# Fixed places for a residual's loads, and other steps of a two-layer trunk moved in time

## The chip, the cores and the metric

The kernel runs on one core of a Trainium2 chip. The metric is device time of one execution in microseconds (us), as the median of three runs. The engines are PE (TensorE, matrix products, with its weight loads PEld), DVE (VectorE), ACT (ScalarE), POOL (GpSimd) and SP (SyncE, which here issues all transfers). Each works through its own instructions in the order in which they were written; they wait for one another by semaphores. PSUM is the memory that PE writes to, in banks of 128 x 512 float32.

## The reference

A trunk of two layers over 1024 tokens of width 1024, all float32. Layer 0 mixes by gated linear attention, layer 1 by sparse attention with a learned index. The change touches layer 1 only. Its core:

```python
# dsa_mixer: 16 heads of 128, 8 index heads of 64, topk = 256, blocks of 128 queries
q = apply_partial_rope(h[..., :o1].reshape(B, L, DSA_HEADS, DSA_HEAD_DIM), cos_h, sin_h)
z = h[..., o3:o4]
rel = relu(einsum('bthd,bsd->bths', qi_b, ki))
score = einsum('bths,bth->bts', rel, wi_b) * INDEX_SCALE      # causal ones only
_, idx = lax.top_k(score, topk)
logits = einsum('bthd,btjd->bthj', q_b, gather(k, idx)) * ATTN_SCALE
o = einsum('bthj,btjd->bthd', softmax(logits), gather(v, idx))
y = (o * silu(z)) @ w_out
# the trunk, after either mixer
x = layer_norm(ALPHA * x + y, ln_g[i], ln_b[i])
x = x + (p[i] @ ple_w[i]) * sigmoid(x @ ple_gate_w[i])
```

All heads share one key and one value of width 128. The top 256 of each query's scores are not gathered: a threshold per query is searched for, and scores below it are masked in `bias_t`.

## The kernel before

**Products in parts.** PE multiplies float32 in three passes: each operand is split in a high and a low part, and a group is high x high, high x low, low x high. The high part is made by ACT (L393, `q<-qf`, `x<-xst`, `u<-uf`; for weights L173, for the probabilities `ph<-PT` at L1463), the low part by DVE behind it (L385; L1461 for `PT`). The layer's weights were split earlier and kept in memory, and come as pairs of transfers `whi`, `wlo` (L165).

**Stages of layer 1.** At 1065 us its projections for keys, values and index begin, then the scores. The tokens are then done in two halves of 512 (half 0 from about 1121 us, half 1 from about 1540). A half consists of 17 slots, numbered -1 to 15, of about 19 to 21 us each. Slot h has as its spine whole blocks of projections (`q` or `z` of a head to come, or an output block `dsa_out` that adds into `y`), and the attention of head h is interleaved: logits `S`, their exponentials into `sq` (ACT, L1417), a turn by DVE (L1423), four stores `sqd` to memory and a load `PT` back in another layout (SP, L1436 and L1446), the split of `PT`, and its products with the values into `o`. A row of sums goes to memory and comes back as `inv`; `uf` is `o` times gate `z` times `inv` (L1515), and its split `u` feeds the output blocks. Behind slot 15 come the last output blocks (`last_outs`), the layer norm of each group of 128 tokens (statistics L795, apply L800, then transposes by PE at L62), and the tail with `p` and the gate (`ple`, `gx`).

**The residual.** `y` starts as alpha times x, which lies transposed in memory (`x2s`, eight tiles of 128 x 512). A tile is loaded into one of two buffers `xst` (L1343), turned by four PE transposes into a PSUM bank from the pool `pb` of three banks (L62), and copied by ACT into `y` (L1370). The loads run one ahead of the transposes. Half 1's input `X` comes by the same loader (`feed_x2`), split instead of turned.

**Top-k.** For the four largest blocks of queries a search bit by bit runs on while half 0 goes: counts on DVE (L1032, 640 to 1024 columns) and, for three blocks, as sign passes on ACT (L1076). The three blocks' scores `sc` are stored first (L1054, `sc_s<-sc`) and read back for the last bit (L1069, `sc<-sc_s`).

**What sets the order.** The program that writes the instructions keeps a clock `fl.now` of planned PE time. `Flow.run` writes the spine and after each piece calls `pace`, which writes every step whose planned time has come (`fl.at`, `after`, `chain`) and lets the pacers step: the weights' loads, and `Background` objects that take one step of a generator each `gap` planned us. `bg` does the top-k, `bg2` the residual. `fl.need(condition)` writes steps ahead of their time until the condition holds. Loads of `p` and their splits are `load_p` (splits `wait` planned us later); the loads of X for half 1 step by `feed_by(feed_x2(X, 1), first time, gap)`.

Of the kernel before, what the change touches and what calls it, by code (L numbers as in the profile page):

```python
# [23 lines left out]
HT = 512  # L24
# [23 lines left out]
class Flow:  # L48
# [23 lines left out]
    def chain(self, *steps):  # L72

        (_, first), rest = steps[0], steps[1:]
        first()
        if rest:
            self.after(rest[0][0], lambda: self.chain((0, rest[0][1]), *rest[1:]))
# [177 lines left out]
def trunk_kernel(ctx, tc, x_tok, x_T, p_T, pos, freq, g_q, g_k, g_v, g_z, g_a, g_a2, g_ba, g_gn, g_o,  # L255
# [79 lines left out]
    later = [key for key, _ in small_keys()] + list(dict.fromkeys(  # L335
        key for key, _ in seq if key[0] in ("dq", "dz", "do") or key[:2] in (("p", 1), ("t", 1))))
    W = Weights(nc, wp, seq, dp, fl.after)
    bg, bg2, bg3 = Background(), Background(), Background()
    fl.pacers += [W.pace, bg.pace, bg2.pace, bg3.pace]


    negs = cp.tile([128, 128], F32, name="negs")
# [38 lines left out]
    def pbank():  # L381
        return psum[0].tile([128, 512], F32, tag="pb", name="pb", bufs=psum[1])
# [4 lines left out]
    def split(hi, lo, src, done=None):  # L387

        def second():
            lo_part(lo, src, hi)  # L390
            if done:
                done()
        chain((0, lambda: act.activation(hi, src, AF.Copy)), (0.9, second))  # L393
# [377 lines left out]
    def load_p(layer, half, alloc, wait=3.0):  # L771
        P = []
        for k in range(2):
            st = xp.tile([128, HT], F32, tag="xst", name="xst", bufs=2)
            nc.sync.dma_start(st, p_T[layer, k, :, half * HT:half * HT + HT])
            ph, pl = alloc(), alloc()
            after(wait, lambda ph=ph, pl=pl, st=st: split(ph, pl, st))
            P.append((ph, pl))
        return P
# [107 lines left out]
    swap_h = list(range(16, 32)) + list(range(16))  # L887
    swap_i = list(range(8, 16)) + list(range(8)) + list(range(16, 32))

    def rope(x, c, s, swap, tmp, then):  # L890
        ab = []

        def first():
            ab[:] = tmp()[:x.shape[0]], tmp()[:x.shape[0]]
            a, b = ab
            dve.tensor_mul(b, x, c)
            dve.stream_shuffle(a, x, swap)
            dve.tensor_mul(a, a, s)

        def second():  # L900
            dve.tensor_add(x, *ab)
        chain((0, lambda: None), (0.8, first), (1.6, second), (1.2, then))


    def small_head(half, X, f32t, alloc, qalloc, tmp, spsum, kih, kil, res):
# [402 lines left out]
    def small_tile(tag, dt=F32, bufs=2):  # L1308
        return l1.tile([128, HT], dt, tag=tag, name=tag, bufs=bufs)
# [4 lines left out]
    def q_phase(st, h, X):  # L1314
        def ev(ps):
            qf = small_tile("qf")
            fl.need(lambda: h < 2 or st.get(("A", h - 2)) == 3)
            qh, ql = small_tile("q", F32R, 4), small_tile("q", F32R, 4)

            def done():  # L1320
                st["q", h] = qh, ql
            act.activation(qf, ps, AF.Copy)
            rope(qf[0:32], tabs[0], tabs[1], swap_h, tmp2, lambda: split(qh, ql, qf, done))

        yield from fm_block(("dq", h), X, ev)

# [30 lines left out]
                X.put(*got)  # L1357
            yield

    def residual(y, rows):  # L1360
        for got in rows:
            if got:
                by_token(y, *got)
            yield

    def by_token(y, k, st):
        ps = pbank()
        for t in range(4):
            fl.transpose(ps[:, t * 128:t * 128 + 128], st[:, t * 128:t * 128 + 128], ident)
        act.activation(y[:, :, k * 128:k * 128 + 128], ps.rearrange("p (t c) -> p t c", c=128), AF.Copy,  # L1370
                       scale=ALPHA)

    def attend(st, h, half, ap, sq):

# [149 lines left out]
                                     [store(i) for i in range(nb)], [load(i) for i in range(nb)], [inverse, to_all])]  # L1524

    def dsa_out(st, js, ch, y, norm=None, ahead=1):
        parts = [W.take(("do", j, ch)) for j in js]

        def U(t, b):
            h = 2 * js[0] + b  # L1530
            fl.need(lambda: ("u", h) in st)
            return tuple(x[:, t * 128:t * 128 + 128] for x in st["uhl", h])

        yield from accumulate(parts, U, y, ch, None, norm, ahead)
        if ch:
            st["out"] = 2 * js[-1] + 2
# [23 lines left out]
    def start_topk(n=len(steps)):  # L1560
        fl.req(res.get("n", 0) == n)
        tk = lambda: sp.tile([128, L], F16, tag="tk", name="tk", bufs=2)
        bg.set(topk_steps([4, 5, 6, 7], scs, l1, tk, tk, on_act=(1, 2, 3)), 1.65)
    fl.at(fl.now + 55.0, start_topk)
    v0, v1 = (vT[i][:, 4:].rearrange("p t d -> p (t d)") for i in range(2))
    raw = xp.tile([128, 4, D], F32, tag="y", name="y").rearrange("p a (b t) -> p (a b) t", t=HT)
# [26 lines left out]
    def unit(u, norm=None):  # L1593
        if u[0] == "o":
            return dsa_out(st, u[1], u[2], y, norm, 3 if u == last_outs[1] else 1)
        return (q_phase if u[0] == "q" else dz_phase)(st, u[1], X)

    for half in range(NH):
# [11 lines left out]
        for h, units in enumerate(plan, -1):  # L1610
# [25 lines left out]
                    fl.at(start + 13.0, loads[0])  # L1636
            last_dur = dur
            if h == 15:
                Pt = load_p(1, half, lambda: small_tile("q", F32R, 4), 8.0)
            if h == -1:  # L1640
                rows = x2_tiles(half)
                next(rows)
            elif h == 0:
                y = xp.tile([128, 4, D], F32, tag="y", name="y")
                bg2.set(residual(y, rows), 4.6 if half else 3.3)
            elif h == 4:
                bg2.finish()
            fl.run(*(unit(u) for u in units))
        norm, y_done = norm_steps(y, l1)
        if half == 0:  # L1650
            X = XT()
            feed_by(feed_x2(X, 1), fl.now + 5.0, 3.0)
        for u in last_outs:
            fl.run(unit(u, norm if u == last_outs[-1] else None))
        fl.drain()
        st.clear()
# [74 lines left out]
```

## Time and profile before

| | us |
|---|---|
| median of three runs (2041.94 to 2046.78) | 2044.94 |
| profiled execution | 2044.36 |
| its span in the trace | 2042.6 |
| PE busy in it | 1971.9 |
| DVE busy | 1489.5 |
| ACT busy | 1040.1 |
| mean share of the transfer engines of SP's queue | 67.9% |

Busy times are sums over the span; PE's idle time is the difference to the span, and the view of waits says which semaphore ended it. The granted clock of PE stands beside the windows: 1.00 is 2.4 GHz, a value between 0.5 and 1 is a mean over a window in which part ran at 1.2 GHz. In timelines consecutive instructions of one kind on the same tiles are drawn together (x2), with their summed duration, and the bracket gives idle time before the first and what ended it.

### The profile page before, as it was taken

How to read it: one execution, taken by the hardware profiler on the slowest of the kernel's cores; microseconds unless marked ns; L12 is line 12 of the kernel's file. 1: busy time of each engine (PE TensorE's matmuls, PEld its weight loads, DVE VectorE, ACT ScalarE, POOL GpSimd, SP SyncE). 2: the span in 40 equal slices, each digit the busy share in tenths (PEclk: the TensorE clock that was granted, in tenths of full speed). 3: DMA queues.
4: the chain of work that ended last, by engine and by line, in shares of the span. 5: the costliest groups of instructions: out<-in, count | busy, mean ns of one | idle time of the engine just before them, and what ended most of it. 6: DMA issues, size and time to landing. Idle time of an engine off the chain costs nothing.

```text
span 2042.6 us, 26801 instructions
## 1 busy us (share of the span) xinstructions
PE 1971.9 (97%) x9016; PEld 1616.1 (79%) x9016; DVE 1489.5 (73%) x3037; ACT 1040.1 (51%) x1943; POOL 88.5 (4%) x151
## 2 busy tenths in 40 slices
PE   8899999999899999999999999999999999999999
PEld 6678888887777788888788777888778887878877
DVE  5676666686777787877857978677696887777873
ACT  5564645445465646464445656666432554434432
POOL 0110101010001101010100000000000000000000
PEclk9999999999999999999999999999999999999999
DMA  4457574757856465656557487878856988888774
GB/s 147 172 155 223 167 224 164 223 171 257 286 187 224 146 218 169 223 168 217 179 192 271 152 278 256 302 257 283 276 190 227 333 314 292 299 294 302 256 266 145
DMA packets 173946, 464.96 MB, mean 228 GB/s; under 512 B 20080, under 2 KB 20848, under 8 KB 167664
## 3 DMA queue, kind: packets, MB, share of 16 engines
q1 hardware_dynamic: 173808, 463.25, 67.9%
q8 instruction: 71, 1.16, 0.2%
q14 instruction: 67, 0.55, 0.1%
HBM read 331.18 MB, written 131.99 MB: 227 GB/s over the span
## 4 chain that ended last, share of the span: by engine, by line
PE 75%; DVE 11%; DMA 6%; ACT 5%; issue 2%; SPq 1%; POOLq 0%; ACTq 0%; POOL 0%; DVEq 0%
PE pb L58 55%; PE o L58 7%; PE U L58 6%; PE S L58 5%; DVE wlo L175 1%; DMA wls<-pst 1%; DVE bn L795 1%; DVE sq L1423 1%; DMA sqd<-sq 1%; DMA whi<-whs 1%; DMA xst<-x2s 1%; DMA PT<-sqd 1%; ACT tk L1076 1%; DMA y<-in_x_T 1%; PE oT L62 1%
## 5 line engine op out<-in xcount | busy, mean ns | idle before, releaser
L58 PE MATMUL pb<-x,whi 128*128 128x512 f32 x2272 | 712.5, 395 | 3.7 <-ACT whi L173 2.3
L58 PEld LDWEIGHTS pb<-x,whi 128*128 128x128 f32 x2272 | 418.1, 189 | 84.4 <-ACT whi L173 3.2
L58 PE MATMUL pb<-x,wlo 128*128 128x512 f32 x1136 | 445.1, 392 | 0.5 <-DVE wlo L175 0.5
L58 PE MATMUL pb<-whi,u 128*128 128x512 f32 x1024 | 345.9, 397 | 5.7 <-ACT u L393 4.2
L58 PEld LDWEIGHTS pb<-x,wlo 128*128 128x128 f32 x1136 | 214.3, 189 | 48.7 <-DVE wlo L175 2.7
L175 DVE TENSOR_TENSOR wlo<-wst,whi 128x512 fp32r<-128x512 f32 x296 | 198.2, 686 | 63.1 <-ACT whi L173 62.7
L58 PEld LDWEIGHTS pb<-whi,u 128*128 128x128 f32 x1024 | 193.6, 189 | 47.8 <-ACT u L393 4.8
L173 ACT ACTIVATE whi<-wst 128x512 fp32r<-128x512 f32 x296 | 174.9, 622 | 78.9 <-DMA wst<-in_g_o 19.8
L58 PE MATMUL pb<-wlo,u 128*128 128x512 f32 x512 | 201.6, 394 | 0.0
L209 ACT ACTIVATE phi<-pst 128x512 fp32r<-128x512 f32 x130 | 81.5, 627 | 138.5 <-DMA pst<-in_d_z 34.1
L1417 ACT ACTIVATE sq<-P,mx 128x128 f32<-128x128 f32 (+7 forms) x128 | 99.0, 773 | 86.6 <-DVE mx L1410 60.1
L58 PE MATMUL S<-kT,q 128*128 128x512 f32 (+2 forms) x576 | 122.5, 344 | 0.6 <-DVE q L385 0.6
L1463 ACT ACTIVATE ph<-PT 128x512 fp32r<-128x512 f32 (+1 forms) x160 | 92.7, 601 | 53.5 <-PE o L58 38.4
L1461 DVE TENSOR_TENSOR PT<-PT,ph 128x512 fp32r<-128x512 f32 (+1 forms) x160 | 101.8, 648 | 21.9 <-ACT ph L1463 21.9
L58 PEld LDWEIGHTS S<-kT,q 128*128 128x128 f32 x576 | 100.2, 189 | 19.4 <-DVE mx L1410 1.7
L58 PEld LDWEIGHTS pb<-wlo,u 128*128 128x128 f32 x512 | 97.1, 190 | 18.4
L1076 ACT ACTIVATE tk<-sc,tki 128x768 f16<-128x768 f32 (+2 forms) x90 | 92.8, 1032 | 27.1 <-DVE tki L1085 20.9
L58 PE MATMUL o<-ph,vT 128*128 128x512 f32 (+2 forms) x384 | 101.6, 349 | 4.0 <-ACT ph L1463 4.0
L213 DVE TENSOR_TENSOR pst<-pst,phi 128x512 fp32r<-128x512 f32 x130 | 89.7, 690 | 20.3 <-ACT phi L209 20.2
L1423 DVE STREAM_TRANSPOSE sq<-sq 128x128 f32<-128x128 f32 (+7 forms) x128 | 97.8, 769 | 6.6 <-ACT sq L1417 6.4
L58 PE MATMUL pb<-whi,x 128*128 128x512 f32 x256 | 90.0, 410 | 10.5 <-ACT whi L173 6.1
L1410 DVE CUSTOM_DVE_ANT_0 P<-S,bias 128x512 f32<-128x512 f32 (+3 forms) x128 | 71.2, 561 | 21.1 <-PE S L58 16.7
(311 smaller groups left out, 3282.4 us busy)
## 6 DMA issues: line engine op xcount, KB each, us to landing
whi<-whs SPq DMA_DIRECT2D x130, 512.0 KB
wlo<-wls SPq DMA_DIRECT2D x130, 512.0 KB
sqd<-sq SPq DMA_DIRECT2D x192, 256.0 KB
PT<-sqd SPq DMA_DIRECT2D x48, 1024.0 KB
whs<-phi SPq DMA_DIRECT2D x130, 256.0 KB
wls<-pst SPq DMA_DIRECT2D x130, 256.0 KB
wst<-in_g_v SPq DMA_DIRECT2D x32, 512.0 KB
wst<-in_g_z SPq DMA_DIRECT2D x32, 512.0 KB
```

Source lines behind the costliest of these rows:

```text
L58: self.pe.matmul(out, lhsT, rhs, start=start, stop=stop)
L62: self.pe.transpose(out, in_, ident)
L173: self.nc.scalar.activation(hi[:, c], st[:, c], AF.Copy)
L175: self.nc.vector.tensor_sub(lo[:, c], st[:, c], hi[:, c].bitcast(F32))
L209: self.nc.scalar.activation(hi, st.bitcast(F32), AF.Copy)
L213: self.nc.vector.tensor_sub(st, st.bitcast(F32), hi.bitcast(F32))
L1076: act.activation(junk()[:, :n], scs[j], AF.Sign, bias=cand[:, j:j + 1].bitcast(F32), accum_out=cnt[:, j:j + 1])
L1410: dve.tensor_tensor_reduce(P[:, a:a + e], ps[:, :e], bias_t[T][:, a:a + e], op0=OP.add, op1=OP.min, scale=-ATTN_SCALE, scalar=lim, accum_o ...
L1417: act.activation(to, rows, AF.Exp, scale=-1.0, bias=mx, accum_out=sm[:, t:t + 1])
L1423: dve.transpose(x, x)
L1461: dve.tensor_sub(lo, lo.bitcast(F32), hi.bitcast(F32))
L1463: chain((0, lambda: act.activation(hi, lo.bitcast(F32), AF.Copy)), (0.8, second))
```

## The change

Five edits, all in layer 1:

1. The residual no longer runs as a background generator. In slots 0 to 3 of each half, two tiles are loaded at 2.2 and 2.8 planned us after the slot's start, and their transposes and copies stand 3.6 and 2.0 planned us before its end. An output block needs all eight first.
2. The split of a head's `q` stands 3.0 instead of 1.2 planned us behind the last step of its rotary (DVE L901).
3. The top-k steps every 1.6 instead of 1.65 planned us, and when the last output block begins it pauses for at least 11 planned us.
4. The splits of `p` stand 14 instead of 8 planned us behind their loads.
5. The loads of half 1's input begin 14 instead of 5 planned us behind the end of slot 15, every 2.8 instead of 3.0.

```diff
-        chain((0, lambda: None), (0.8, first), (1.6, second), (1.2, then))
+        chain((0, lambda: None), (0.8, first), (1.6, second), (wait, then))
...
-            rope(qf[0:32], tabs[0], tabs[1], swap_h, tmp2, lambda: split(qh, ql, qf, done))
+            rope(qf[0:32], tabs[0], tabs[1], swap_h, tmp2, lambda: split(qh, ql, qf, done), 3.0)
...
-    def residual(y, rows):
-        for got in rows:
-            if got:
-                by_token(y, *got)
-            yield
+    def residual(st, y, half, ks, start, end):
...
+        for i, k in enumerate(ks):
+            fl.at(start + 0.6 * i, lambda k=k: load(k))
+            fl.at(end - 3.6 + 1.6 * i, lambda k=k: by_token(k))
...
     def dsa_out(st, js, ch, y, norm=None, ahead=1):
+        fl.need(lambda: st.get("y") == NK)
...
-        bg.set(topk_steps([4, 5, 6, 7], scs, l1, tk, tk, on_act=(1, 2, 3)), 1.65)
+        bg.set(topk_steps([4, 5, 6, 7], scs, l1, tk, tk, on_act=(1, 2, 3)), 1.6)
...
-                Pt = load_p(1, half, lambda: small_tile("q", F32R, 4), 8.0)
-            if h == -1:
-                rows = x2_tiles(half)
-                next(rows)
-            elif h == 0:
+                Pt = load_p(1, half, lambda: small_tile("q", F32R, 4), 14.0)
+            if h == 0:
                 y = xp.tile([128, 4, D], F32, tag="y", name="y")
-                bg2.set(residual(y, rows), 4.6 if half else 3.3)
-            elif h == 4:
-                bg2.finish()
+            if 0 <= h < 4:
+                residual(st, y, half, (2 * h, 2 * h + 1), start + 2.2, start + dur)
...
-            feed_by(feed_x2(X, 1), fl.now + 5.0, 3.0)
+            feed_by(feed_x2(X, 1), fl.now + 14.0, 2.8)
         for u in last_outs:
+            if u == last_outs[-1]:
+                bg.due = max(bg.due, fl.now + 11.0)
             fl.run(unit(u, norm if u == last_outs[-1] else None))
```

How three places read in the order of the instructions. First SP's queue in slot 0 of half 0 (`xst<-x2s` are the residual's loads, `sc_s<-sc` stores of the top-k), before:

```order
L1343 DMA xst<-x2s 128x512
L1489 DMA inv<-row 128x512
L1436 DMA sqd<-sq 32x4x512 x4
L1054 DMA sc_s<-sc_9849 128x768
L165 DMA whi<-whs 128x1024
L165 DMA wlo<-wls 128x1024
L1054 DMA sc_s<-sc_9850 128x896
L1343 DMA xst<-x2s 128x512
L1054 DMA sc_s<-sc_9851 128x1024
L1446 DMA PT<-sqd 128x2048
```

and in the changed kernel:

```order
L1366 DMA xst<-x2s 128x512 x2
L1496 DMA inv<-row 128x512
L165 DMA whi<-whs 128x1024
L165 DMA wlo<-wls 128x1024
L1054 DMA sc_s<-sc_9849 128x768
L1443 DMA sqd<-sq 32x4x512 x4
L1054 DMA sc_s<-sc_9850 128x896
L1054 DMA sc_s<-sc_9851 128x1024
L1453 DMA PT<-sqd 128x2048
```

The slot's two residual loads now stand together, ahead of the stores of scores and of the four `sqd` stores; two of these stores of scores follow the `sqd` stores, and no residual load stands before `PT`.

Second DVE at the end of half 0, where its last attention head closes, from behind the split of the first `PT` of the piece on (`q<-xst` are the low parts of `p`, `x<-xst` of half 1's input, L1032 are counts of the top-k, 768 and more columns after the reload), before:

```order
L385 TENSOR_TENSOR q<-xst,q 128x512 x2
L1032 TENSOR_SCALAR tk,tkf<-sc_9848,tki 128x640
L754 TENSOR_TENSOR y<-pb,y 128x512
L1461 TENSOR_TENSOR PT<-PT,ph 128x4x96
L1082 TENSOR_TENSOR tki<-tkf 128x4
L1083 SCALAR_TENSOR_TENSOR tki<-tki 128x4
L1085 TENSOR_SCALAR tki<-tki 128x4
L1461 TENSOR_TENSOR PT<-PT,ph 128x2x4x64
L1506 TENSOR_TENSOR z<-z,inv 128x512
L1515 TENSOR_TENSOR uf<-o,z 128x4x4x32
L385 TENSOR_TENSOR x<-xst,x 128x512
L385 TENSOR_TENSOR u<-uf,u 128x512
```

and in the changed kernel, from behind the same `PT` on:

```order
L1072 TENSOR_SCALAR tki<-tki 128x3
L754 TENSOR_TENSOR y<-pb,y 128x512
L1468 TENSOR_TENSOR PT<-PT,ph 128x4x96
L1032 TENSOR_SCALAR tk,tkf<-sc_9848,tki 128x640
L1468 TENSOR_TENSOR PT<-PT,ph 128x2x4x64
L1032 TENSOR_SCALAR tk,tkf<-sc_9849,tki 128x768
L1513 TENSOR_TENSOR z<-z,inv 128x512
L1522 TENSOR_TENSOR uf<-o,z 128x4x4x32
L1032 TENSOR_SCALAR tk,tkf<-sc_9850,tki 128x896
L385 TENSOR_TENSOR q<-xst,q 128x512 x2
L385 TENSOR_TENSOR u<-uf,u 128x512
```

The low parts of `p` moved from behind the first `PT` to behind `uf`, half 1's input left the piece, and two counts of a later round now stand here, one of them between `uf` and the low part of `u`. On SP the three reloads that these counts read stood behind the loads of half 1's input; now the first stands right behind `inv`, and the other two one pair of weight loads later.

Third ACT in a slot of half 1 in which a head's `q` is made (`qf` is the copy from PSUM, `q<-qf` the high part, `ph<-PT` the probabilities' high parts), before:

```order
L1463 ACTIVATE ph<-PT 128x512 x2
L1322 ACTIVATE qf<-pb 128x512
L393 ACTIVATE q<-qf 128x512
L1463 ACTIVATE ph<-PT 128x512 x2
L1463 ACTIVATE ph<-PT 128x384
L1463 ACTIVATE ph<-PT 128x512
```

and in the changed kernel:

```order
L1470 ACTIVATE ph<-PT 128x512
L1322 ACTIVATE qf<-pb 128x512
L1470 ACTIVATE ph<-PT 128x512 x2
L393 ACTIVATE q<-qf 128x512
L1470 ACTIVATE ph<-PT 128x512
L1470 ACTIVATE ph<-PT 128x384
L1470 ACTIVATE ph<-PT 128x512
```

The split `q<-qf` stood right behind `qf`, with four `ph` behind it; now two `ph` stand between the two, and three behind.

## Rows read from the trace of the kernel before

**Rows 1.** section 1 of the page: engine, busy us, share, instructions

```profile
PE 1971.9 (97%) x9016; PEld 1616.1 (79%) x9016; DVE 1489.5 (73%) x3037; ACT 1040.1 (51%) x1943; POOL 88.5 (4%) x151
```

**Rows 2.** waits of PE, stretches 1150:1200, 1440:1540, 1660:1960, 1960:2043 in turn

```profile
PE pb L62 <- DMA xst<-x2s: 4.8, 1, 4.8
...
PE pb L58 <- ACT u L393: 2.7, 1, 2.7
PE S L62 <- DVE y L800: 2.4, 3, 1.5
PE o L58 <- DVE PT L1461: 1.5, 1, 1.5
...
PE o L58 <- ACT ph L1463: 4.0, 3, 1.8
...
PE pb L58 <- DVE y L754: 1.4, 1, 1.4
```

**Rows 3.** windows: us, busy of PE, PEld, DVE, ACT, POOL, clock, DMA share, GB/s

```profile
1180.00:1200.00 20.00, 15.20 (x73) 12.55 (x72) 12.80 (x34) 7.52 (x17) 0.00 (x0) 0.91 0.98 323
1460.00:1480.00 20.00, 15.74 (x60) 12.19 (x59) 12.17 (x23) 5.41 (x10) 0.00 (x0) 0.83 0.88 313
1480.00:1500.00 20.00, 17.50 (x76) 13.75 (x75) 19.28 (x41) 6.70 (x11) 3.85 (x8) 0.91 0.51 173
```

**Rows 4.** timeline of PE, slot 0: start, duration, group, idle before and releaser

```profile
1192.40 1.09 PE L62 MATMUL pb<-ident,xst 128*128 128x128 f32 x4 [4.80 <-DMA xst<-x2s]
1193.14 1.20 PE L58 MATMUL pb<-x,whi 128*128 128x512 f32 x2
...
1195.59 0.63 PE L58 MATMUL pb<-x,whi 128*128 128x512 f32 x2
```

**Rows 5.** timeline of SP's queue, slot 0 of half 0

```profile
1178.53 2.71 SPq L1436 DMA_DIRECT2D sqd<-sq  x4
...
1185.07 0.42 SPq L1343 DMA_DIRECT2D xst<-x2s  x1
```

**Rows 6.** ACT's copies of the residual, and its top-k passes (page, section 5)

```profile
L1370 ACT ACTIVATE y<-pb x16: 574/581/600, 1168.4 to 1653.3; 128x512 f32<-128x512 f32 x16
...
L1076 ACT ACTIVATE tk<-sc,tki 128x768 f16<-128x768 f32 (+2 forms) x90 | 92.8, 1032 | 27.1 <-DVE tki L1085 20.9
```

**Rows 7.** timeline of DVE, end of half 0

```profile
1463.98 1.29 DVE L385 TENSOR_TENSOR q<-xst,q 128x512 fp32r<-128x512 f32 x2
...
1469.09 0.69 DVE L1515 TENSOR_TENSOR uf<-o,z 128x512 f32<-128x512 f32 x1 [0.28 <-PE o L58]
...
1472.54 0.68 DVE L385 TENSOR_TENSOR u<-uf,u 128x512 fp32r<-128x512 f32 x1
```

**Rows 8.** timeline of ACT, end of half 0

```profile
1471.27 0.63 ACT L393 ACTIVATE x<-xst 128x512 fp32r<-128x512 f32 x1 [5.86 <-DMA xst<-x2s]
1471.80 0.61 ACT L393 ACTIVATE u<-uf 128x512 fp32r<-128x512 f32 x1
```

**Rows 9.** timeline of SP's queue, end of half 0

```profile
1460.90 0.33 SPq L1489 DMA_DIRECT2D inv<-row  x1
...
1464.70 0.98 SPq L1343 DMA_DIRECT2D xst<-x2s  x2
```

**Rows 10.** timeline of PE, end of half 0

```profile
1472.47 0.79 PE L58 MATMUL pb<-whi,u 128*128 128x512 f32 x1 [2.72 <-ACT u L393]
```

**Rows 11.** timeline of DVE, last norm of half 0

```profile
1487.92 1.01 DVE L1032 TENSOR_SCALAR_CACHE_REDUCE tk<-sc,tki 128x768 f16<-128x768 f32 x1
...
1492.16 1.14 DVE L1032 TENSOR_SCALAR_CACHE_REDUCE tk<-sc,tki 128x896 f16<-128x896 f32 x1
```

**Rows 12.** timelines of ACT and of PE, half 1

```profile
1686.49 0.63 ACT L393 ACTIVATE q<-qf 128x512 fp32r<-128x512 f32 x1 [5.37 <-DVE qf L901]
...
1687.69 0.73 PE L58 MATMUL o<-ph,vT 128*128 128x512 f32 x2 [1.78 <-ACT ph L1463]
```

**Rows 13.** instructions on tile S, PE, 1680 to 1720: min/median/max ns, first and last start

```profile
L58 PE MATMUL S<-kT,q x24: 278/362/397, 1696.4 to 1702.1; 128*128 128x512 f32 x12, 128*128 128x384 f32 x6, 128*128 128x256 f32 x6
```

More of the change, by code (lines that the diff above doesn't have):

```diff
@@ L337, in trunk_kernel @@
     W = Weights(nc, wp, seq, dp, fl.after)
-    bg, bg2, bg3 = Background(), Background(), Background()
-    fl.pacers += [W.pace, bg.pace, bg2.pace, bg3.pace]
+    bg, bg3 = Background(), Background()
+    fl.pacers += [W.pace, bg.pace, bg3.pace]
     negs = cp.tile([128, 128], F32, name="negs")
@@ L888, in trunk_kernel, with rope @@
     swap_i = list(range(8, 16)) + list(range(8)) + list(range(16, 32))
-    def rope(x, c, s, swap, tmp, then):
+    def rope(x, c, s, swap, tmp, then, wait=1.2):
         ab = []
@@ L1358, in feed_x2, with load, by_token @@
             yield
-    def residual(y, rows):
-        for got in rows:
-            if got:
-                by_token(y, *got)
-            yield
[L1366 to L1371, printed above, removed]
+    def residual(st, y, half, ks, start, end):
+        tiles = {}
+        def load(k):
+            tiles[k] = xp.tile([128, HT], F32, tag="xst", name="xst", bufs=2)
+            nc.sync.dma_start(tiles[k], x2s[k, :, half * HT:(half + 1) * HT])
+        def by_token(k):
+            ps = pbank()
+            for t in range(4):
+                fl.transpose(ps[:, t * 128:t * 128 + 128], tiles[k][:, t * 128:t * 128 + 128], ident)
+            act.activation(y[:, :, k * 128:k * 128 + 128], ps.rearrange("p (t c) -> p t c", c=128), AF.Copy,
+                           scale=ALPHA)
+            st["y"] = k + 1
+        for i, k in enumerate(ks):
+            fl.at(start + 0.6 * i, lambda k=k: load(k))
+            fl.at(end - 3.6 + 1.6 * i, lambda k=k: by_token(k))
     def attend(st, h, half, ap, sq):
```

## Prediction

> **What bounds the kernel now.** I read the busy shares first. TensorE (PE) is busy 1971.9 us of a span of 2042.6 us [rows 1], so only some 71 us of idle time can go, over both layers, and a faster kernel is one whose PE waits less or whose clock falls less. The change touches layer 1 alone (from about 1065 us on), so I then read the view of waits for PE there, stretch by stretch [rows 2]. Six lines are worth naming: one wait of 4.8 us of a transpose for the load of the residual, one of 2.7 us for `u`, three for the norm's `y` with 2.4 us, one of 1.5 us for `PT`, three for `ph` in half 1 with 4.0 us, and one of 1.4 us for `y` near the end. Then the table of 20 us windows: in layer 1 only a few show a granted clock below 1.00, among them the three printed [rows 3], where it is 0.91, 0.83 and 0.91. They hold the first four of these lines. So a wait there costs twice: itself, and matmuls at the lower of the two clock levels (1.2 instead of 2.4 GHz) right behind it. The timelines of these places give the terms below.
>
> **Residual in fixed places, slot 0 of half 0.** PE stands 4.80 us until 1192.40, for a tile `xst` [rows 4]. The order of SP tells why: the load was issued at 1185.07, behind four stores `sqd` (1178.53, 2.71 us of issuing) and stores of the scores [rows 5], with the transfer engines 98% busy at 323 GB/s [rows 3]. After the wait a pair of matmuls takes 1.20 us, and by 1195.59 a pair takes 0.63 again [rows 4]. Some 2.9 us thus ran at half speed, which costs 1.4 us. In the changed order the two loads of slot 0 stand before the scores' stores and the `sqd` stores, and their transposes stand at the slot's end, 3.6 and 2.0 planned us before it. The load then has over 10 us where it needed 7.3 (1185.07 to 1192.40). The wait goes, and with it the low clock: 4.8 + 1.4 = 6.2 us. The bounds: at most 6.2; at least 0, if the wait turns up at another load. The `PT` load behind them has fewer transfers ahead of it than before, so I see none that is late next.
>
> The same edit puts eight pairs of transposes (four slots in each half) at slot ends. PE's work is the same; ACT's copy takes 0.58 us [rows 6]. I count this as nothing, since PE has other matmuls between the two and before the slot's end, and ACT is half idle. If the cover fails, a slot's first matmul waits for a PSUM bank; that is the third rival.
>
> **The end of half 0.** Here four edits meet: p's splits later, half 1's loads later, and the top-k's reloads and counts, at a gap of 1.6 instead of 1.65, now ahead of them. Before, PE waits 1.54 us for `PT`, since VectorE (DVE) does two splits of `q` (1.29 us) and a count first [rows 7], and then 2.72 us for `u` until 1472.47 [rows 10]: ACT has done `u` only behind an `x` split whose load arrived at 1471.27 [rows 8], 6.6 us after SP began to issue it at 1464.70 [rows 9]. In the changed order of DVE `PT` comes ahead of the splits, so the 1.54 goes, and `u` on ACT is ahead of `x`. But before `u`'s low part DVE now does a count over 768 columns and one over 896, each of which waits for a reload, and the two `q` splits. Worked out with the 6.6 us: the 768 reload is issued behind `inv` (1460.90 [rows 9]) at about 1461.3 and is there at 1467.9; count 1.01 (as in [rows 11]), `z` and `uf` 1.3, so `uf` ends at 1470.2 where it ended at 1469.78 [rows 7]. The 896 reload, two weight loads later, is there at about 1470; count 1.14 [rows 11], splits 1.29, `u` 0.68 [rows 7]: `u` low is ready at about 1473.3. Before, that part began at 1472.54 and ended at 1473.2. PE thus resumes 1.7 us earlier, does two matmuls and waits again, and is past this place 0.3 us earlier or level. I take 0.3 us, and the low clock (0.83 over 1460 to 1480) stays. Bounds: a transfer 1.5 us later makes it a loss of 1; one that lands at once leaves only DVE's own work and brings `u` low to about 1472, a gain of 1.5, and 4.5 if the clock then holds.
>
> The row's 6.6 us is for 256 KB at a DMA share of 0.88. The Trainium skill (DMA: Bandwidth & Descriptors, Anatomy of one DMA) puts a transfer at about 2.0 us fixed plus its bytes over 436 GB/s, which by estimate is 2.6 us here and 3.1 us for the 896 reload; the trace does not agree, its queue is full. By that rule the end of half 0 would gain 1.5 instead of 0.3 us and the whole would come to 2031.3 us, part of the first rival.
>
> **The last norm of half 0.** Between statistics and applies DVE does top-k counts of 1.01 and 1.14 us [rows 11]; PE waits 2.4 us for `y` meanwhile [rows 2], and the clock of 1480 to 1500 is 0.91 [rows 3], which is up to 0.09 x 20 = 1.8 us. After, the pause keeps the top-k away until the applies are through: 2.15 us less on the chain that PE waits for. But DVE is busy 19.28 of 20 us there [rows 3], and the counts left over follow right behind. So I take the 2.4 us of waiting and nothing for the clock. Bounds: 4.2 (both), and 0 if the work comes back as waits behind the norm.
>
> **q's split later.** In three slots of half 1 ACT holds the split `q<-qf` for 5.37 us, waiting for DVE's rotary, with four `ph` queued behind it; PE waits 1.78 us at 1687.69 for the first of them [rows 12]. The lines of [rows 2] say 4.0 us in three. Now two `ph` stand between `qf` and the split. I take 3.5 us, leaving 0.5 for what remains of the late `ph`; bounds 0 and 4.0. Below nothing it does not go: `q` is first read at 1696.4 [rows 13], and its low split, two DVE instructions after 1687.69, has 7 us to spare before 1.8 us are added.
>
> These three waits come at a regular distance, one in about 106 us. The Trainium skill (Perfetto Trace Analysis, Identifying the Most-Contended Engine) says that a gap that repeats on the engine that should be full can mean too little SBUF or PSUM for the next tile. By that rule the order of ACT would not matter and the 3.5 us would stay: 2036.0 us, the second rival's upper neighbour. The trace speaks against it: ACT idles in the row, and what releases it is DVE.
>
> At the end of half 1 the wait of 1.4 for `y` [rows 2] loses the p splits (1.29) ahead of it, which now stand ahead of the last `PT` instead; I count 0, between -0.8 and +1.4.
>
> **Sum.** 6.2 + 0.3 + 2.4 + 3.5 = 12.4 us. The profiled execution took 2044.36 us (its span 2042.6 and 1.8 around it); 2044.36 - 12.4 = 2032.0. The median of the runs is 0.6 above that execution, so 2032.5 us.
>
> **Rivals.**
> First, all terms at their upper ends: the tail's transfers land early and the clock holds in all three places, 6.2 + 4.5 + 4.2 + 4.0 = 18.9 us, or 2026 us. For it: the three low clocks each come right behind a wait. Against it: the changed order itself puts DVE behind two loads at the tail. 0.16.
> Second, only the residual's stall goes, 6.2 us, or 2038.7 us: DVE, at 19.28 of 20 us, hands each wait on. For it: [rows 3]; against it: in half 1 ACT is idle when PE waits. 0.18. With the repeated gap kept and the rest as summed, 2036.0 us: 0.08.
> Third, slower. In eight slots the two transposes take two of three PSUM banks at the slot's end, and the next slot's first matmul waits for ACT's copies, which stand behind a top-k pass of 1.03 us [rows 6]: 1.03 + 2 x 0.58 = 2.2 us a slot, 17.6 in all, so 2044.9 - 12.4 + 17.6 = 2050 us. It decides from 16.5 / 8 = 2.1 us a slot. Against it: PE's list of waits in the slots that did such copies before shows none for them [rows 2, 6]. 0.05 for this, and 0.05 for a half of it, about 2041 us.
> The forecast keeps 0.48.
>
> **Chances and range.** Two kernels are told apart from about 0.2%, 4.1 us. Faster: the forecast, the first, the second and its neighbour, 0.90, less 0.05 for cases of these that add up to under 4.1 us: 0.85. Within: 0.10. Slower: 0.05. The range takes in the first rival's time and the second's with the half-size collision: 2025.5 to 2041. The forecast's own range is 2028 to 2036.
>
> **What would show it.** Right: no wait for `xst` in slot 0 and clock 1.00 there; at the end of half 0 no wait for `PT`, and a second, short wait for `u` low; waits for `y` at the norm under 0.5 us; no `ph` wait over 0.5 us in half 1; PE's busy time falls by 1 to 3 us, its idle time by some 10. Wrong: PE waits for `sqd`, `PT` or a bank in slots 1 to 4; the tail's waits grow beyond 4.3 us; or waits for `gx` after the norm grow by as much as those for `y` shrink.

## The result and the profile after

The changed kernel takes 2029.66 us (median of four runs, 2028.81 to 2030.01) beside 2045.86 for the kernel before on the same chip: ratio 0.9923, 95% interval 0.9906 to 0.994. It is 16 us faster, and the time lies 2.8 us under the forecast. The profiled execution has a span of 2027.8 us, 14.8 less than before.

Where the time went is best read by pieces. Both traces hold 9016 matmuls and transposes on PE, so the start of the n-th can be compared. The table gives, for pieces cut at fixed numbers n (their times in the trace of before stand ahead), by how much each piece is shorter (-) or longer than before. Work until 1180 is nearly all the same code; there single executions differ by up to 4 us either way, and I do not read that column. All behind it together is 12.5 us shorter in the changed kernel.

| us against before | until 1180 | 1180 to 1214 (the tile) | 1214 to 1295 | 1295 to 1450 | end of half 0, to 1490 | norm, to 1527 | half 1 |
|---|---|---|---|---|---|---|---|
| changed kernel | -2.5 | -5.7 | +0.9 | +1.3 | -0.6 | -3.6 | -4.8 |
| first edit alone | -3.5 | -5.8 | -2.5 | +1.2 | -4.3 | 0.0 | -4.8 |
| second edit alone | -2.7 | +0.1 | +1.1 | +0.9 | -1.6 | 0.0 | -1.3 |
| edits three to five | -2.4 | -1.1 | -0.8 | -0.2 | 0.0 | -3.6 | +1.9 |
| changed, no pause | -4.0 | -5.7 | -0.7 | +1.3 | 0.0 | +2.0 | -6.0 |
| changed, no second edit | +2.6 | -5.5 | -1.0 | -0.2 | -1.2 | -3.6 | -5.3 |
| before, one step 0.3 earlier | +0.6 | +0.8 | 0.0 | 0.0 | -1.7 | 0.0 | -2.3 |
| first edit, half 0 alone | -2.1 | -4.7 | -2.5 | +1.2 | -4.7 | 0.0 | -0.3 |
| changed, gap 1.65 | -2.1 | -5.1 | -1.7 | +1.6 | -5.9 | -3.1 | -4.9 |
| hold, splits at 20 | -3.9 | -5.7 | +0.9 | +1.3 | -1.6 | -5.5 | -6.1 |
| the same, no second edit | -0.1 | -5.5 | -0.7 | -0.2 | -1.7 | -5.4 | -4.8 |
| hold, splits at 16, no second edit | +1.9 | -5.9 | -1.0 | -0.2 | -6.7 | -4.6 | -6.1 |
| the same, gap 1.65 | -2.7 | -5.6 | -2.5 | +1.2 | -6.7 | -2.7 | +4.5 |

Three things have to be known for reading it. First, the planner's clock puts the transposes that waited for the tile in slot 1 of half 0 (their load is issued in slot 0), and the piece to 1295 ends in slot 6; "slot 0" below is the place of that wait. Second, with the first edit eight of the residual's transposes more fall between 1214 and 1295, and five fewer between 1180 and 1214, where longer products take their numbers. Counted without these transposes, the piece to 1214 is 6.3 us shorter in the changed kernel and 6.5 with the first edit alone; that to 1295, with 0.7 us taken off for the eight, is 2.0 longer and 1.4 shorter. Third, the row "before, one step 0.3 earlier" has the instructions of before up to half 1, and still differs by +0.8 and -1.7 us in two pieces, as the low clocks there lasted differently; a single difference of that size in one profiled execution shows nothing by itself.

Busy time answers to [rows 1]. PE's fell by 2.4 us and the span by 14.8, so nearly all of it was waiting:

```profile
PE 1969.5 (97%) x9016; PEld 1619.3 (80%) x9016; DVE 1488.6 (73%) x3037; ACT 1040.3 (51%) x1943; POOL 88.9 (4%) x151
```

PE's waits in the changed kernel, answering to [rows 2], first over 1200 to 1440, then 1440 to 1540, then 1660 to 1960; from 1150 to 1200 there is none (columns: total us, times, longest):

```profile
PE o L58 <- DVE PT L1468: 2.1, 1, 2.1
PE S L62 <- DVE sm L1476: 1.7, 1, 1.7
...
PE pb L58 <- DVE u L385: 2.7, 1, 2.7
PE pb L58 <- ACT u L393: 1.7, 1, 1.7
PE pb L58 <- DVE gx L385: 1.1, 3, 0.5
PE S L62 <- DVE y L800: 0.4, 1, 0.4
...
PE pb L58 <- ACT u L393: 1.4, 1, 1.4
PE o L58 <- DVE PT L1468: 0.6, 1, 0.6
PE pb L58 <- DVE y L754: 0.2, 1, 0.2
```

The waits for the residual's tile in half 0 (4.8 us), for `ph` and nearly all for `y` are gone. The 1.4 us for `u` in the last stretch are not new: in before they stand at 1969.53, behind that window. New are 2.1 us for `PT` and 1.7 us for `sm` in half 0, and 2.7 us for the low part of `u`. The windows that answer to [rows 3], with two new ones (columns as there):

```profile
1180.00:1200.00 20.00, 20.00 (x105) 16.87 (x104) 17.44 (x47) 13.83 (x32) 0.00 (x0) 1.00 0.85 311
1240.00:1260.00 20.00, 17.87 (x79) 14.57 (x78) 14.93 (x39) 11.23 (x26) 0.00 (x0) 0.91 0.76 278
1460.00:1480.00 20.00, 15.67 (x60) 12.15 (x59) 15.62 (x31) 1.37 (x3) 1.48 (x4) 0.83 0.75 277
1480.00:1500.00 20.00, 18.94 (x96) 14.62 (x94) 19.42 (x36) 15.12 (x23) 2.82 (x4) 1.00 0.51 182
1940.00:1960.00 20.00, 17.73 (x70) 13.48 (x70) 12.22 (x20) 5.77 (x10) 0.00 (x0) 0.91 0.68 254
```

The low clock of slot 0 and of the norm went (0.91 to 1.00 twice), that of the end of half 0 stayed at 0.83, and two new ones came: at 1240 behind the wait for `PT`, and at 1940 at the end of half 1. On balance the clock gave nothing in layer 1. PE and then DVE at the end of half 0, answering to [rows 7] and [rows 10]:

```profile
1463.89 0.50 PE L58 MATMUL pb<-whi,u 128*128 128x512 f32 x1 [1.66 <-ACT u L393]
1467.30 1.22 PE L58 MATMUL pb<-whi,u 128*128 128x512 f32 x2 [2.67 <-DVE u L385]
```

```profile
1462.49 0.69 DVE L1522 TENSOR_TENSOR uf<-o,z 128x512 f32<-128x512 f32 x1
1464.28 1.15 DVE L1032 TENSOR_SCALAR_CACHE_REDUCE tk<-sc,tki 128x896 f16<-128x896 f32 x1 [1.10 <-DMA sc<-sc_s]
...
1465.35 1.29 DVE L385 TENSOR_TENSOR q<-xst,q 128x512 fp32r<-128x512 f32 x2
1466.56 0.68 DVE L385 TENSOR_TENSOR u<-uf,u 128x512 fp32r<-128x512 f32 x1
```

This is the queue that the prediction worked out: `uf`, a wait for the reload, the count over 896 columns, the two splits of `p`, and only then the low part of `u`, for which PE stands 2.67 us. The reload of the 896 columns is the first of these two on SP's queue; the count that reads it starts 8.3 us after its issue:

```profile
1455.94 2.00 SPq L1069 DMA_DIRECT2D sc<-sc_s  x2
```

### The profile page after: what moved, and what is told of

It is laid out like the page before. It is cut to its first block, busy times and chain, and to the rows that moved or that the text cites. A ratio compares the mean times of both kernels' runs of the same rounds, so it can differ in the third digit from the quotient of the medians.

```text
span 2027.8 us, 26796 instructions
## 1 busy us (share of the span) xinstructions
PE 1969.5 (97%) x9016; PEld 1619.3 (80%) x9016; DVE 1488.6 (73%) x3037; ACT 1040.3 (51%) x1943; POOL 88.9 (4%) x151
## 4 chain that ended last, share of the span: by engine, by line
PE 75%; DVE 10%; DMA 6%; ACT 5%; issue 2%; SPq 1%; POOL 0%; POOLq 0%; ACTq 0%; DVEq 0%
PE pb L58 55%; PE o L58 7%; PE U L58 6%; PE S L58 6%; DMA pst<-in_d_z 1%; DVE wlo L175 1%; DVE bn L795 1%; DMA wls<-pst 1%; DMA sqd<-sq 1%; DMA y<-in_x_T 1%; PE oT L62 1%; DVE pst L213 1%; DMA xst<-x2s 1%; ACT phi L209 1%; PE tr L58 1%
## 5 line engine op out<-in xcount | busy, mean ns | idle before, releaser
L702 ACT ACTIVATE junk<-o 128x512 bf16<-128x512 f32 x32 | 19.1, 597 | 128.1 <-DVE ot L700 128.1
```

## The experiments

Twelve kernels were run, each beside the kernel before on the same chip. The theory after the first reading of the traces: the prediction's terms for slot 0, the end of half 0 and the norm stand; half 1's gain is the second edit's, as predicted; and one of the edits makes the new waits in half 0.

**The first edit alone.** Only the residual's loads and turns are moved.

> The kernel before with the first edit alone (residual's loads and turns in fixed places). Theory: the 4.8 us wait for a residual tile in slot 0 and the half clock behind it go, nothing else moves: 6 us faster than before (about 2039), waits for ph in half 1 still 4.0 us in three, waits for y in the norm still about 2.4 us. Rival: the new waits of slots 1 to 14 in the changed kernel (2.1 us for PT with a low clock behind it, 1.7 us for sm) come from the turns at the slots' ends; then they are here too and the gain is only about 2 us.

2027.11 us beside 2042.89, ratio 0.9922 (0.9909 to 0.9936): the whole gain of the change by itself. The expectation of 6 us was wrong. Slot 0 gave 5.8, as expected, but the end of half 0 gave 4.3 and half 1 4.8 besides. The rival was half right: PE waits 1.63 us for `sm` at 1329.89, where it waited 0.16 before, and no 2 us for `PT`. In half 1 (1660 to 1960) the waits for `ph` are gone without q's split having moved; what stands there of PE's waits are the two that stand behind 1960 in before (1.45 and 1.44 us there):

```profile
PE pb L58 <- ACT u L393: 1.4, 1, 1.4
PE pb L58 <- DVE y L754: 1.4, 1, 1.4
```

The order shows how. In this kernel ACT's instructions at the place of the third order piece ahead of the prediction read `ph`, `qf`, `ph`, `q<-qf` and four `ph`: one `ph` has crossed `q<-qf`, though no number of the second edit was changed. At the end of half 0 PE (first fence) waits 1.04 us for `u` where it waited 2.72 [rows 10], since the `x` load on which ACT waited ahead of `u` (second fence) arrived 4.1 us after its issue at 1455.20, not 6.6 [rows 8, 9] (that load took 5.8 and 5.9 us in the second edit alone and in the kernel with one step 0.3 earlier, whose queue there is that of before, and 3.1 with the first edit in half 0 alone); and the clock stays at 1.00 (third fence):

```profile
1460.48 0.50 PE L58 MATMUL pb<-whi,u 128*128 128x512 f32 x1 [1.04 <-ACT u L393]
```

```profile
1459.28 0.63 ACT L393 ACTIVATE x<-xst 128x512 fp32r<-128x512 f32 x1 [5.66 <-DMA xst<-x2s]
```

```profile
1460.00:1480.00 20.00, 17.27 (x72) 13.13 (x72) 18.01 (x34) 3.98 (x7) 3.85 (x8) 1.00 0.87 331
```

**The second edit alone.**

> The kernel before with the second edit alone (q's split later). Theory: the three waits for ph in half 1 (4.0 us, 5.4 us with the matmuls behind them) go, and the wait for the residual's tile stays: 4 to 5 us faster than before. Rival: in half 0 the later split stands behind sign passes of the top-k on ACT, DVE waits for it, and PE for DVE: new waits for PT or sm of 2 to 5 us in half 0, so that nothing or at most 3 us is left.

2040.51 us, ratio 0.9991 (0.9981 to 1.0001): no difference that can be told. Half 1 gained 1.3 us, not 4 to 5: the waits for `ph` went, but waits for the low part `PT` behind it took their place (1660 to 1960; of the 1.9 us for `y`, 1.4 stood behind 1960 in before):

```profile
PE o L58 <- DVE PT L1461: 2.2, 3, 1.0
PE pb L58 <- DVE y L754: 1.9, 2, 1.4
```

In half 0 it lost 2.0 us (+1.1 and +0.9 in the table). The rival held.

**Edits three to five alone.**

> The kernel before with edits three to five alone (top-k gap 1.6 and pause, p's splits and half 1's loads later). Theory: the end of half 0 gains 0.2 us, the norm 3.6 us (waits for y under 0.5 us, clock 1.00 there): 3 to 4 us faster than before. Rival: the other gap of the top-k makes the new waits of slots 1 to 14; then they are here, and the gain is 0 to 1 us.

2038.24 us, ratio 0.9976 (0.9965 to 0.9986), and the norm gained 3.6 us, as in the changed kernel. No new wait for `PT` of 2 us appeared in half 0, so the rival, that the other gap by itself makes it, fell; one of 0.85 us for `sm` is new, at 1200.70. It lost 1.9 us in half 1: at its end PE waits 0.63 us for the last `PT`, behind p's later splits, and 1.45 for `u` close behind, and the clock of that window falls to 0.91.

**The changed kernel without the pause.**

```diff
-            if u == last_outs[-1]:
-                bg.due = max(bg.due, fl.now + 11.0)
```

> The changed kernel without the pause of the top-k at the last norm. Theory: the pause is what the norm gained from; counts stand again between statistics and applies, PE waits over 2 us for y and the clock falls behind it: 2.5 to 4 us slower than the changed kernel (about 2033). Rival: the norm gained from the earlier counts of 768 to 1024 columns and from half 1's loads coming later; then within 1 us of the changed kernel.

2035.61 us, ratio 0.9958 (0.9945 to 0.997), which stands to 0.9923 as 7 us slower, where 2.5 to 4 were expected. The profiled execution was its fastest (2031.57), and behind 1180 it is 3.4 us longer than the changed kernel's. The norm is 5.6 us longer than with the pause (+2.0 against -3.6). Its waits (1478 to 1540) are those for `y` again, and more behind them:

```profile
PE pb L58 <- DVE gx L385: 2.0, 3, 1.2
PE S L62 <- DVE y L800: 1.8, 3, 0.9
PE pb L58 <- DVE rt L385: 1.0, 1, 1.0
```

**The changed kernel without the second edit.**

```diff
-            rope(qf[0:32], tabs[0], tabs[1], swap_h, tmp2, lambda: split(qh, ql, qf, done), 3.0)
+            rope(qf[0:32], tabs[0], tabs[1], swap_h, tmp2, lambda: split(qh, ql, qf, done))
```

> The changed kernel without its second edit (q's split again 1.2 planned us behind the rotary). Theory: the first edit has already taken the waits for ph in half 1 away, since the turns at the ends of slots move a group of products across a slot's boundary, so the second edit gives nothing there and costs in half 0 (the wait of 2.1 us for PT with its low clock, 1.7 us for sm): within 1 us of the first edit alone or faster, 0 to 3 us faster than the changed kernel. Rival: the second edit is what freed ph, and without it 4 us of waits for ph come back: 3 to 4 us slower than the changed kernel.

2028.46 us, ratio 0.993 (0.9918 to 0.9943): the changed kernel's time. By pieces half 1 is 0.5 us better than with the edit, and the two pieces from 1214 to 1450 are 3.4 us better (-1.2 against +2.2). Some 1.6 us of this is the low clock at 1243.62, which does not come with every such wait (last section); what is the edit's is 1.72 us for `sm` at 1415.76, where 0.27 is left without it, and 0.4 us for `PT` (1.73 left of 2.13). So beside the first edit the second costs in half 0, and in half 1 it does not give the forecast's 3.5: taking it out gains 0.5 us in this pair and loses 1.3 in the pair with the hold below. A row shows how it costs: at 1413.43 DVE waits for ACT's high part of `q`, with the `sm` that PE needs three instructions behind; ACT does it only at 1412.78, behind two sign passes, although the rotary had ended at 1411.31. From the changed kernel, ACT, DVE and PE in turn:

```profile
1411.76 1.03 ACT L1076 ACTIVATE tk<-sc,tki 128x896 f16<-128x896 f32 x1
...
1412.78 0.61 ACT L393 ACTIVATE q<-qf 128x512 fp32r<-128x512 f32 x1
```

```profile
1410.64 0.67 DVE L901 TENSOR_TENSOR qf<-rt 32x512 f32<-32x512 f32 x1
...
1413.43 0.69 DVE L385 TENSOR_TENSOR q<-qf,q 128x512 fp32r<-128x512 f32 x1 [1.52 <-ACT q L393]
...
1414.64 0.87 DVE L1032 TENSOR_SCALAR_CACHE_REDUCE tk<-sc,tki 128x640 f16<-128x640 f32 x1
...
1415.44 0.18 DVE L1476 RECIPROCAL sm<-sm 128x4 f32<-128x4 f32 x1
```

```profile
1415.76 0.27 PE L62 MATMUL S<-ident,sm 128*4 128x128 f32 x1 [1.72 <-DVE sm L1476]
```

**The kernel before with one step 0.3 planned us earlier.** How can the first edit reach slots 5 to 15 of half 1, where it has no instruction? The planner's clock, printed at each slot's start, says: in before, slots 4, 5, 6, 7 of half 1 start at 1472.46, 1497.05, 1520.36, 1544.95 planned us; with the first edit at 1473.10, 1496.41, 1521.00, 1544.31. One group of three matmuls (3 x 512 / 2400 = 0.64) crosses the boundary of slot 3, and every later boundary up to slot 14 moves by it, forth and back. All steps of a slot are planned from its start, so `ph` changes places with `qf`. This edit makes the same starts without touching the residual:

```diff
-                spread(pvs, start + lead + 2.9, dur - lead - 2.4)
+                spread(pvs, start + lead + (2.9 - 0.3 if half and h == 3 else 2.9), dur - lead - 2.4)
```

> The kernel before with one number changed: in slot 3 of half 1 alone the products of the probabilities stand 0.3 planned us earlier. The planned starts of slots 4 to 14 then move by 0.6 us, odd and even ones in opposite directions, to where the first edit puts them. Theory: this displacement alone takes the three waits for ph away: 4 to 5.7 us faster than before, all of it in half 1, with the 4.8 us wait for the residual's tile still there. Rival: the first edit's gain in half 1 came from its loads or from its turns at the slots' ends; then the waits for ph stay at 4.0 us and the time is that of before within 1 us.

2040.86 us beside 2045.25, ratio 0.9984 (0.9975 to 0.9993). Half 1 gained 2.3 us. Two of the three waits for `ph` went; of the first there remained 1.2, and 0.7 for `PT` (1660 to 1960):

```profile
PE o L58 <- ACT ph L1463: 1.2, 1, 1.2
PE o L58 <- DVE PT L1461: 0.7, 1, 0.7
```

So the displacement by itself takes two away, and the rival (nothing without the residual's edit) fell. It is not the whole of the 4.8 us.

**The first edit in half 0 alone.** Half 1 keeps the background residual and before's planned starts.

```diff
-            if h == -1:
+            if h == -1 and half:
...
+            if 0 <= h < 4 and half == 0:
+                residual0(st, y, half, (2 * h, 2 * h + 1), start + 2.2, start + dur)
```

> The kernel before with the first edit in half 0 alone; half 1 keeps the residual as a background step, and its planned starts of slots are those of before. Theory: half 0 gains what the first edit alone gains there (some 11 us: the wait for the residual's tile with its low clock, 2.5 us in slots 1 and 2, and the low clock at the half's end), and the three waits for ph (4.0 us) stay in half 1: 10 to 12 us faster than before, 4 to 5 us slower than the first edit in both halves. Rival: half 1 gains from what happens in half 0 (its loads and order), then 15 us as the first edit alone.

2032.88 us beside 2041.83, ratio 0.9956 (0.9943 to 0.9968), 9 us faster. Half 1 is that of before within 0.3 us, with its three waits (1660 to 1960; the last two lines stand behind 1960 in before):

```profile
PE o L58 <- ACT ph L1483: 3.8, 3, 1.6
PE pb L58 <- ACT u L393: 1.4, 1, 1.4
PE pb L58 <- DVE y L754: 1.4, 1, 1.4
```

With the run before, this settles that half 1's gain is half 1's residual edit, at least in good part through the planned starts, and does not come over from half 0.

**The changed kernel with the top-k's old gap.**

```diff
-        bg.set(topk_steps([4, 5, 6, 7], scs, l1, tk, tk, on_act=(1, 2, 3)), 1.6)
+        bg.set(topk_steps([4, 5, 6, 7], scs, l1, tk, tk, on_act=(1, 2, 3)), 1.65)
```

> The changed kernel with the top-k's gap of before, 1.65 instead of 1.6. Theory: the wait of 2.1 us for PT with its low clock and that of 1.7 us for sm in half 0 come from where the top-k's counts and sign passes fall with the other gap; they shrink below 1 us each: 3 us faster than the changed kernel, up to 4 where the end of half 0 keeps its clock. Rival: q's later split makes them, whatever the gap; then within 1 us of the changed kernel.

2021.18 us beside 2041.83, ratio 0.9897 (0.9884 to 0.9911): some 5 us faster than the changed kernel. The wait of 2.1 us for `PT` and its low clock went (1214 to 1295: -1.7 instead of +0.9), and that for `sm` at 1415.76 fell to 0.40, both under 1 us as expected. But another wait for `sm` came, of 1.48 us at 1332.29, at the same matmul as the 1.63 of the first edit alone, which has this gap (1295 to 1450: +1.6). The end of half 0 kept its clock: -5.9. In half 0 (1200 to 1440) there stand:

```profile
PE S L62 <- DVE sm L1476: 1.9, 2, 1.5
PE o L58 <- DVE PT L1468: 0.8, 2, 0.5
```

**Top-k held over the end of half 0 and the norm.** In this and the next kernel the last counts come behind the norm, and p's splits 20 planned us behind their loads.

```diff
+                if half == 0:
+                    fl.at(start + dur - 6.0, lambda: setattr(bg, "due", fl.now + 16.0))
-                Pt = load_p(1, half, lambda: small_tile("q", F32R, 4), 14.0)
+                Pt = load_p(1, half, lambda: small_tile("q", F32R, 4), 20.0)
```

> The changed kernel with the top-k held from 6 planned us before the end of slot 15 of half 0 until behind the norm, and p's splits 20 instead of 14 planned us behind their loads. Theory: u's low part then no longer stands behind a reload, a count and two splits; the wait of 2.7 us for it goes, the wait for u's high part (1.7 us) stays or shrinks, and the clock at the end of half 0 stays 1.00: 4 to 6 us faster than the changed kernel. Rival: the low clock comes with the wait for u's high part alone, and DVE, full in the norm, hands the work on: 1 to 2 us faster at most.

2025.24 us, ratio 0.9914 (0.9901 to 0.9928), some 2 us faster than the changed kernel, within the intervals, where 4 to 6 were expected. The wait for `u`'s low part went and that for its high part fell to 0.9, as the theory has it; but PE now waits for the low part of `p`, and the clock falls there:

```profile
1474.45 0.53 PE L58 MATMUL pb<-q,whi 128*128 128x512 f32 x1 [3.18 <-DVE q L385]
...
1475.21 1.05 PE L58 MATMUL pb<-q,whi 128*128 128x512 f32 x2
```

> As the run with the top-k held and p's splits later, but without the second edit (q's split at 1.2). Theory, by adding the pieces: the end of half 0 as in that run, the slots of half 0 without the new wait for PT and its low clock: 5 to 9 us faster than the changed kernel, about 2021. Rival: ph waits of 4 us in half 1 come back without the second edit, and it is no faster than the run with the top-k held and the second edit.

2025.6 us, ratio 0.9915 (0.9902 to 0.9929): the same. The 4 us in half 1 did not come back, and the expected extra gain is 1.7 us by the pieces, too little to be told.

**The same with p's splits at 16, without the second edit.**

> Without the second edit, top-k held over the end of half 0 and the norm, and p's splits 16 planned us behind their loads (20 in the run before with a hold). Theory: the wait of 3.2 us for p's low part, which the hold with 20 brought, goes, as the split now stands right behind u's; the wait for u of about 1 us stays: 3 to 6 us faster than that run, about 2020. Rival: DVE is full there and the same wait comes back for y: no faster than that run.

2021.7 us beside 2041.83, ratio 0.9895 (0.9881 to 0.991), 4 us better than the run before, as expected. The wait for `p` is gone and the clock at the end of half 0 is 1.00:

```profile
1463.71 0.50 PE L58 MATMUL pb<-whi,u 128*128 128x512 f32 x1 [0.75 <-ACT u L393]
1481.06 0.77 PE L62 MATMUL S<-ident,y 128*128 128x128 f32 x5 [0.71 <-DVE y L800]
```

From 1180 on it is 24.4 us shorter than before, where the changed kernel is 12.5. With the changed kernel at gap 1.65 it is the best of all that were run; the two differ by less than their intervals.

**The same with the gap of 1.65.**

> As the run with the hold and p's splits at 16, with the top-k's gap at 1.65. Theory: the slots of half 0 lose the wait of 1.7 us for PT that the gap of 1.6 left there, a gain of 1 to 2 us over that run. Rival: another wait of that size appears elsewhere in half 0, within 0.7 us of it.

2029.94 us, ratio 0.9933 (0.9921 to 0.9946): 8 us slower than at 1.6. The slots of half 0 behaved as the theory says only in part (-2.5 and +1.2): the wait for `PT` went, and one of 1.62 us for `sm` came, as with the first edit alone. What decided lies elsewhere: the top-k, held and at the slower gap, was not done when half 1 began, the rest was written out there at once, and PE waited 4.06 us for `q` behind it, with the clock at 0.83 over 1540 to 1560:

```profile
1546.12 3.98 PE L58 MATMUL S<-kT,q 128*128 128x384 f32 x12 [4.06 <-ACT q L393]
```

## Why the prediction was right, and where its reasons were not

The time lies 2.8 us under the forecast of 2032.5, in the forecast's own range. Between the profiled executions all pieces behind 1180 gave 12.5 us, where the sum had 12.4, and the rest lies ahead of them, in code that is nearly all unchanged. That the sum agrees so well is luck: its steps, in order, were off by more.

*Slot 0*: 6.2 us forecast; 5.7 measured by number, 6.3 without the displaced transposes (5.8 and 6.5 with the first edit alone). No wait for the tile, clock 1.00.

*The turns at slots' ends*: forecast at nothing, and in none of the traces does PE wait over 0.15 us for one of ACT's copies of a turn. What this step missed is that the turns also shift the planner's clock by a group, and with it all later slots of half 1.

*The end of half 0*: 0.3 forecast, 0.6 measured, which are the same within what unchanged code differs by there (1.7), and by the mechanism that was worked out: PE resumed on `u`'s high part, did two matmuls and waited again behind the reload, the count and the splits. Of the two values for a load weighed there, the measured 6.6 us was the nearer, as the 8.3 us of the 896 reload show. By the rule of the Trainium skill (DMA: Bandwidth & Descriptors, Anatomy of one DMA), which the page gives for transfers that GpSimd issues and not SP as here, it would have taken an estimated 3.1 us; the trace does not agree. But the runs show that this place was worth 6 to 7 us (-5.9 and -6.7), once the chain is short enough that the clock holds; the forecast's bound of 4.5 was too low. Over all fourteen traces the clock fell at this place in the nine whose longest wait there is 2.0 to 3.2 us, and held in the five where it is at most 1.4.

*The norm*: 2.4 forecast, 3.6 measured. The term was mis-sized: the waits for `y` fell from 2.4 to 0.4, and the low clock, put at nothing, went as well (0.91 to 1.00). The counts that follow did not come back as waits: those for `gx` were 1.1 before and after. Without the pause the piece is 5.6 us longer, so the pause is what did it.

*q's split later*: 3.5 forecast for half 1, and half 1 is 4.8 shorter; but the step as the prediction put it, that two `ph` ahead of the split free PE, failed. The second edit alone brought 1.3 us in half 1, since waits for `PT` took the place of those for `ph`, and taking it out of the changed kernel lost nothing. The gain is the first edit's. Too few buffers, weighed there as the other reading of these repeated waits, was no better: two of the three went by moving one step by 0.3 planned us, with no buffer added. The rule of the Trainium skill (Perfetto Trace Analysis, Identifying the Most-Contended Engine) that a gap that repeats can mean too little SBUF or PSUM is thus not borne out here.

*The end of half 1*: forecast 0 between -0.8 and +1.4. The wait for `y` fell from 1.4 to 0.2; the last `PT`, behind p's splits, brought a wait of 0.62 and, behind it and the old one for `u`, a low clock (0.91). Without the second edit, and without the pause, the same two waits came with no low clock (1.00 over 1940 to 1970).

*Half 0's slots* were not in the sum. They lost 2.2 us by number, 3.3 without the displaced transposes: a wait for `PT` of 2.13 us with a low clock, and one for `sm` of 1.72. Two terms too small (norm, half 1) and one left out thus nearly cancelled. Which edits make these waits is read from the same matmuls in the other traces (us of waiting; a dash is under 0.15):

| | before | first edit | second edit | edits three to five | changed | changed, no second edit | changed, gap 1.65 |
|---|---|---|---|---|---|---|---|
| `PT`, at 1243.62 in the changed kernel | - | - | - | - | 2.13 | 1.73 | 0.27 |
| `sm`, at 1329.89 with the first edit alone | 0.16 | 1.63 | 1.07 | - | - | - | 1.48 |
| `sm`, at 1415.76 in the changed kernel | - | - | - | 0.27 | 1.72 | 0.27 | 0.40 |

The first wait needs the first edit and the gap of 1.6 together. The second comes at the gap of 1.65 with the first edit, and at 1.07 us with the second edit too. The third, but for 0.4 us, needs the gap of 1.6 and the second edit.

*The signs.* Of those for being right all came but one: the second wait for `u` was 2.67 us and not short. PE's busy time fell by 2.4 us, its idle time by 12.4. Of those for being wrong, PE did wait for `PT` in slots 1 to 4 (the 2.13 us stand in slot 4), and the waits at the end of half 0 came to 4.33 us, at the bound of 4.3.

Of the rivals, the first (all at their upper ends, 2026 us) was nearest to what the parts can give, but it needed another gap or a hold. The second did not occur, since the norm and half 1 gained too, nor did the third, slower one.

What stays open: why the first of the three waits for `ph` remained, in part, where only the planned starts were moved (over 1640 to 1700 ACT's exponentials wait 12.4 us for the stores `sqd` there, 11.2 in before and 3.1 with the first edit alone, so the place of the residual's loads may have its own share; no run took it apart); and why the load at the end of half 0 came 2.5 us sooner with the first edit alone.

## What to carry to other kernels

In a schedule that is planned from running starts, an edit's reach is not its own instructions: compare the order of all engines to the end of the program, and the planned starts, before a gain far behind the edit is given to another edit. Run each edit by itself and leave each out once: here one of five gave the whole gain, one gave nothing that can be told, and a change of 0.05 in one gap was worth 5 us (the changed kernel without the first edit, and the fourth and fifth edits by themselves, were not run). When a wait is removed, look at what is next in the same engine's queue: `ph` gave way to `PT`, `u` to the splits ahead of it.

## What was not expected of the hardware

Behind waits of about 2 us the clock did not follow the wait. In the changed kernel it fell to the 1.2 GHz level behind one wait of 2.13 us (the window of 1240 to 1260 is 0.91). Without the pause, PE waits the same 2.13 us at the same matmul and the clock stays at 2.4 GHz (window 1.00); the two kernels have the same instructions in the same order on PE and ACT throughout, and on DVE outside 1476 to 1532. First the changed kernel, then the one without the pause:

```profile
1243.62 0.50 PE L58 MATMUL o<-PT,vT 128*128 128x512 f32 x1 [2.13 <-DVE PT L1468]
...
1244.77 1.05 PE L58 MATMUL pb<-whi,u 128*128 128x512 f32 x2
```

```profile
1242.20 0.50 PE L58 MATMUL o<-PT,vT 128*128 128x512 f32 x1 [2.13 <-DVE PT L1468]
...
1243.00 0.62 PE L58 MATMUL pb<-whi,u 128*128 128x512 f32 x2
```

The piece from 1214 to 1295 is 1.6 us longer with the low clock (+0.9 against -0.7). At the end of half 1 it is the same: behind 0.62 and 1.44 us close together the clock fell in the changed kernel, and behind 0.62 and 1.45 without the pause it did not. It also stayed up behind one wait of 2.04 us in the changed kernel with the gap of 1.65 (1494.37, the pairs behind it at 0.62):

```profile
1494.37 0.50 PE L58 MATMUL pb<-gx,whi 128*128 128x512 f32 x1 [2.04 <-DVE gx L385]
...
1494.95 0.62 PE L58 MATMUL pb<-z,whi 128*128 128x512 f32 x2
```

So whether a wait of about 2 us costs itself or nearly double could not be told from the wait, and differs between executions of the same instructions; a term of the sum that hangs on it needs both values as bounds. It also means that a low clock seen in one profiled execution is no proof that an edit made it.

Work whose instructions were not changed (until 1180) differed between single executions by -4.0 to +2.6 us; against terms of 1 to 6 us only pieces between fixed instructions can be compared.
